# Seven-product down chunks in x's dead buffers, rotary angles on GpSimd, and one more Strassen pair in a two-layer trunk kernel

## The chip, the cores and the metric

The kernel runs on one core of one Trainium2 chip. The metric is device time in microseconds (us) of one execution, lower is better; several executions give a median. Engines are called by the profile's names: PE (TensorE, matrix multiply), PEld (its weight load), DVE (VectorE), ACT (ScalarE), POOL (GpSimd) and SP (the queue from which all DMAs of this kernel are issued).

## The reference, cut to what matters

Two layers, 256 positions, width 1024, fp32. The change touches the feed-forward halves (`ffn`, four in all) and the rotary tables of layer 1.

```python
def swiglu(h, w_gate, w_up, w_down):            # w_gate, w_up: 1024 x 2816; w_down: 2816 x 1024
    return (jax.nn.silu(h @ w_gate) * (h @ w_up)) @ w_down

def rope_tables(positions):
    ang = positions.astype(jnp.float32)[..., None] * inv_freq
    return jnp.cos(ang), jnp.sin(ang)

for i in range(2):
    x = x + 0.5 * swiglu(rmsnorm(x, ffn1_norm[i]), ffn1_w_gate[i], ffn1_w_up[i], ffn1_w_down[i])
    ...   # one input projection, self attention (relative bias in layer 0, differential with rotary in layer 1),
    ...   # cross attention into mem (256 x 1024), one output projection, added to x
    x = x + 0.5 * swiglu(rmsnorm(x, ffn2_norm[i]), ffn2_w_gate[i], ffn2_w_up[i], ffn2_w_down[i])
```

## The kernel before, in words

**Three passes per product.** Every dense product in fp32 is made of three PE matmuls of 128x512 in a reduced type: the high part of x by the high part of the weight, high by low, low by high (`dense`, lines 496, 499, 502). The weights arrive by DMA in fp32 as chunks of 128 x 2048 values (1 MB) in tile `raw` (three buffers). ACT casts a chunk to its high part `hi` (`split_hi`, line 326), DVE subtracts to get the low part `lo` (`split_lo`, line 344). `hi` and `lo` have four buffers each (pool `whl`), taken in turn, so a chunk can be split as soon as the buffer four takes back is free.

**Stages.** Each of the four `ffn` calls, (layer, which) = (0,1), (0,2), (1,1), (1,2), has a gate/up stage of 11 groups of 256 columns, two chunks a group, 24 matmuls a chunk, and then a down stage of 11 chunks, 24 matmuls a chunk. After a group, `evac` makes silu(gate)*up, transposes it in blocks (DVE), sends it through DRAM to turn it (`hd` out, `hr` back, lines 627 and 632) and splits it for the down stage (`ht`). The last three down chunks are done output quarter by output quarter, so that each quarter of x is finished, normalised and turned (`finish`, `prep_half`) while PE works on the next.

**Products by Strassen's scheme.** Where `PAIR[l, nm]` names a group, that group and the next are computed with seven products of four 12-matmul blocks instead of eight (Winograd's form): `pair_forms` makes four sums of x on DVE and splits them, `split_lo` makes sums of weight blocks (`wsum`, line 338), `pair_sums` adds the products up. Before, three of the four gate/up stages do it (from group 3) and the first, (0,1), does not. Where `SEVEN[l, nm]` names down chunks, each takes seven products instead of eight (`seven_item`, `seven_forms`, `seven`); such a chunk needs seven `hi`/`lo` quarters and so two of the four buffers; after the last one `seven_sums` adds the products into x (nine DVE operations, lines 690 and 695). The chunks are 1, 4, 6 in (0,2) and (1,1), and 1, 4, 7 in (1,2).

**Who sets the order.** All instructions are issued in an order that a planner at build time (class `Flow`) works out: it keeps a clock from fixed costs (a 128x512 matmul 0.216 us, a hop between engines 0.22 us), and threads yield the time or condition at which they go on. Each engine then runs its own instructions in that order and waits on semaphores. Ordinary threads go ahead of the idle ones (`loader`, `split_hi`, `split_lo`, `rope_setup`); many wait until DVE or ACT is free within `SLACK` = 0.4 us by the planner's clock. A split of the chunk that PE is working on does not wait for that.

**Rotary angles.** `rope_setup` computes the angles by a chain of 95 small dependent DVE operations on 128x64 or smaller (argument reduction in five pieces), then two `Sin` on ACT and 16 small DVE products. It is an idle thread and each operation goes only when DVE has nothing to do, so that the chain spreads from 125 us to 640 us of the profile; the tables are first used at 688 us. `memory_turn` and `memory_prep` bring `mem` in and turn it during (0,1).

Of the kernel before, what the change touches and what calls it, by code (L numbers as in the profile page):

```python
# [12 lines left out]
F32 = mybir.dt.float32  # L13
F32R = mybir.dt.float32r
# [6 lines left out]
P = 128  # L21
# [121 lines left out]
def kernel(  # L143
# [101 lines left out]
    class Item:  # L245
# [3 lines left out]
        def __init__(self, raws, uses=8, w=1):  # L249
# [3 lines left out]
            self.n, self.frees, self.takes, self.gives = 1, 1, 0, 0  # L253
# [15 lines left out]
    hl_left = [NHL]  # L269
    dma_free = [2.3]  # L270
# [94 lines left out]
    SEVEN = {(0, 1): (), (0, 2): (1, 4, 6), (1, 1): (1, 4, 6), (1, 2): (1, 4, 7)}  # L365
    PAIR = {(0, 1): None, (0, 2): 3, (1, 1): 3, (1, 2): 3}
# [10 lines left out]
    def seven_item(it):  # L377
# [3 lines left out]
        it.n, it.uses, it.takes, it.gives = 2, 7, 4, 4  # L381
# [48 lines left out]
    def plan_ffn(l, nm, wg, wu, wd):  # L430
# [58 lines left out]
    def dense(ps, xh, xl, ready, c, need, start, stop):  # L489
# [14 lines left out]
        if c.uses == 0:  # L504
            hl_left[0] += c.n
        return flow.pe(T_MM)
# [88 lines left out]
    def ffn(l, nm, xt, gc_next):  # L595
# [5 lines left out]
        def evac(g, ps, end, gives=None):  # L601
# [27 lines left out]
            g2.give()  # L629
            yield g2.has()  # L630
# [206 lines left out]
        nxt = None if gc_next is None else Xt(nm == 2 and PAIR[l + 1, 1] is not None)  # L837
# [27 lines left out]
        if nm == 1:  # L865
            table_hint(AF.Exp)
        for tb in range(2):
# [55 lines left out]
    def memory_turn():  # L923
        yield lambda: at[0] >= 8
        ss = const.tile([P, 2, 4], F32, name="mss")
        for q in range(4):
# [22 lines left out]
    def memory_prep():  # L949
        yield g2.has(8)  # L950
# [102 lines left out]
    def calm(n, extra=0.0):  # L1053
        t = flow.dve(n, extra) + 0.3
        return lambda: flow.now >= t and flow.free["V"] <= flow.now

    def rope_setup():
# [13 lines left out]
        nc.vector.tensor_copy(pf, pi)  # L1071
        yield calm(2)
        for tb in range(2):
            nc.vector.tensor_scalar(out=ang[:, tb * 32:(tb + 1) * 32], in0=invf, scalar1=pf[:, tb:tb + 1],
                                    scalar2=None, op0=ALU.mult)
            yield calm(n)
# [3 lines left out]
        nc.vector.tensor_copy(hi, hr.bitcast(F32))  # L1080
        yield calm(n)
        nc.vector.tensor_sub(lo, ang, hi)
        yield calm(n)
# [595 lines left out]
```

## Time and profile before

| | |
|---|---|
| median of 3 runs | 961.64 us (959.97 to 965.21) |
| profiled execution, its own time | 962.03 us |
| its span in the trace | 960.3 us |
| mean granted TensorE clock | 0.998 of 2.4 GHz |
| PE, DVE, ACT, POOL busy | 99%, 84%, 60%, 7% of the span |

The span runs from the first to the last instruction; 1.7 us of the profiled execution's time lie around it. A busy PE is not a PE at its peak, since matmuls overlap and their ends are modelled; the starts of successive matmuls tell how fast PE takes them.

### The profile page before, as it was taken

What the parts mean: (1) busy time and instruction counts of PE and PEld (TensorE: products, weight loads), DVE (VectorE), ACT (ScalarE), POOL (GpSimd) and SP (SyncE); (2) the same over time, 40 slices, a digit from 0 to 9 for tenths busy, and PEclk for the clock granted to TensorE, in tenths of its full rate; (3) what the DMA queues carried; (4) which work ended last, traced back from release to release, by engine and by line L of the source; (5) the groups of instructions that cost most, each with busy time, mean ns of one, the idle gap of its engine ahead of it and who ended that gap; (6) DMA issues with size and microseconds to landing.
All of it is one profiled execution on the core that took longest, in us unless ns stands there. A gap on an engine that the chain in (4) does not pass through costs nothing.

```text
span 960.3 us, 13252 instructions
## 1 busy us (share of the span) xinstructions
PE 948.0 (99%) x4489; PEld 776.9 (81%) x4489; DVE 806.0 (84%) x1532; ACT 577.8 (60%) x1100; POOL 63.1 (7%) x65
## 2 busy tenths in 40 slices
PE   8999999999999999999999999999999999999998
PEld 6888888888877888888888888887787788888886
DVE  6867777788877889979989988798989888997885
ACT  6655555566676656556646655554676866665651
POOL 1000000022110100000000000000334100000000
PEclk9999999999999999999999999999999999999999
DMA  8988868486435387786756678666541375688761
GB/s 275 332 256 273 278 229 274 154 272 210 158 107 174 92 262 226 233 289 221 234 184 201 219 231 263 221 234 224 187 165 45 126 223 183 211 258 261 240 230 44
DMA packets 169294, 204.02 MB, mean 212 GB/s; under 512 B 9674, under 2 KB 144395, under 8 KB 169227
## 3 DMA queue, kind: packets, MB, share of 16 engines
q1 hardware_dynamic: 169226, 203.18, 65.7%
q8 instruction: 35, 0.57, 0.2%
q14 instruction: 33, 0.26, 0.1%
HBM read 188.99 MB, written 14.16 MB: 212 GB/s over the span
## 4 chain that ended last, share of the span: by engine, by line
PE 87%; DVE 8%; DMA 2%; ACT 1%; SPq 1%; issue 1%; DVEq 0%; ACTq 0%
PE gu L502 14%; PE gu L499 14%; PE gu L496 14%; PE acc L496 8%; PE acc L502 8%; PE acc L499 8%; DVE lo L344 3%; PE pj L502 3%; PE pj L499 3%; PE pj L496 3%; PE pair_m L502 2%; PE pair_m L499 2%; PE pair_m L496 2%; PE xtp L509 1%; PE S L1320 1%; PE AV L1401 1%
## 5 line engine op out<-in xcount | busy, mean ns | idle before, releaser
L326 ACT CAST hi<-raw 128x512 fp32r<-128x512 f32 (+1 forms) x469 | 338.2, 771 | 160.9 <-DMA raw<-in_ffn_w_up_dram 43.4
L344 DVE TENSOR_TENSOR lo<-raw,hi 128x512 fp32r<-128x512 f32 (+1 forms) x469 | 393.0, 873 | 45.4 <-ACT hi L326 44.6
L502 PE MATMUL gu<-hi,xl 128*128 128x512 f32 x608 | 236.9, 390 | 0.0
L496 PE MATMUL gu<-hi,xh 128*128 128x512 f32 x608 | 236.8, 389 | 0.0
L499 PE MATMUL gu<-lo,xh 128*128 128x512 f32 x608 | 236.7, 389 | 0.0
L502 PEld LDWEIGHTS gu<-hi,xl 128*128 128x128 f32 x608 | 114.1, 188 | 23.7
L499 PEld LDWEIGHTS gu<-lo,xh 128*128 128x128 f32 x608 | 114.1, 188 | 23.6
L496 PEld LDWEIGHTS gu<-hi,xh 128*128 128x128 f32 x608 | 114.2, 188 | 23.5
L499 PE MATMUL acc<-lo,ht 128*128 128x512 f32 x280 | 110.1, 393 | 2.0 <-DVE lo L344 2.0
L496 PE MATMUL acc<-hi,ht 128*128 128x512 f32 x280 | 110.0, 393 | 0.0
L502 PE MATMUL acc<-hi,ht 128*128 128x512 f32 x280 | 109.9, 393 | 0.0
L502 PE MATMUL pj<-hi,xl 128*128 128x512 f32 x160 | 64.5, 403 | 0.0
L499 PEld LDWEIGHTS acc<-lo,ht 128*128 128x128 f32 x280 | 52.9, 189 | 13.7 <-DVE lo L344 2.9
L499 PE MATMUL pj<-lo,xh 128*128 128x512 f32 x160 | 63.6, 397 | 0.0
L496 PE MATMUL pj<-hi,xh 128*128 128x512 f32 x160 | 63.5, 397 | 0.0
L502 PEld LDWEIGHTS acc<-hi,ht 128*128 128x128 f32 x280 | 53.0, 189 | 11.0
L496 PEld LDWEIGHTS acc<-hi,ht 128*128 128x128 f32 x280 | 53.0, 189 | 10.9
L641 ACT CAST ht<-hr 128x512 fp32r<-128x512 f32 x35 | 21.7, 619 | 65.2 <-DMA hr<-hd 65.1
L326 ACT CAST hi<-wsum 128x512 fp32r<-128x512 f32 x84 | 49.2, 621 | 15.7 <-DVE wsum L338 12.3
L344 DVE TENSOR_TENSOR lo<-wsum,hi 128x512 fp32r<-128x512 f32 x84 | 53.0, 682 | 0.0
L610 ACT ACTIVATE sil<-gu,xr 128x256 f32<-128x256 f32 x76 | 35.7, 469 | 24.6 <-PE gu L502 24.1
L643 DVE TENSOR_TENSOR ht<-hr,ht 128x512 fp32r<-128x512 f32 x35 | 24.0, 687 | 26.1 <-ACT ht L641 26.0
(215 smaller groups left out, 1297.6 us busy)
## 6 DMA issues: line engine op xcount, KB each, us to landing
raw<-in_ffn_w_down_dram SPq DMA_DIRECT2D x176, 256.0 KB, 4.3
raw<-in_ffn_w_gate_dram SPq DMA_DIRECT2D x86, 512.0 KB, 4.6
raw<-in_ffn_w_up_dram SPq DMA_DIRECT2D x86, 512.0 KB, 5.7
raw<-in_w_in_dram SPq DMA_DIRECT2D x32, 512.0 KB, 5.9
hd<-hb SPq DMA_DIRECT2D x44, 256.0 KB, 4.9
hr<-hd SPq DMA_DIRECT2D x44, 256.0 KB, 3.7
raw<-in_w_out_dram SPq DMA_DIRECT2D x8, 1024.0 KB, 4.9
raw<-in_w_mem_kv_dram SPq DMA_DIRECT2D x4, 1024.0 KB, 5.6
```

Of the source, the lines that this page charges most:

```text
L326: nc.scalar.copy(out=it.part(0, q, w), in_=src())
L344: nc.vector.tensor_sub(it.part(1, q, w), src(), it.part(0, q, w).bitcast(F32))
L496: nc.tensor.matmul(out=ps, lhsT=xh, rhs=wh, start=start, stop=False)
L499: nc.tensor.matmul(out=ps, lhsT=xh, rhs=wl, start=False, stop=False)
L502: nc.tensor.matmul(out=ps, lhsT=xl, rhs=wh, start=False, stop=stop)
L509: nc.tensor.transpose(out=dst, in_=src, identity=flip if flipped else ident)
L610: nc.scalar.activation(sil, ps[tb][:, 0:256], AF.Silu, scale=xt.r[tb])
L641: nc.scalar.copy(out=hi, in_=src)
L643: nc.vector.tensor_sub(lo, src, hi.bitcast(F32))
L1320: nc.tensor.matmul(out=ss[e][:, pr, :nk], lhsT=q[rows, pr, :], rhs=k[rows, pr, :], start=i == 0, stop=i == len(passes) - 1)
L1401: nc.tensor.matmul(out=av[64 * e:64 * e + 64, pr, :], lhsT=vsrc(kb, pr, e), rhs=pts[e][:, pr, kb, :], start=(kb == 0), stop=(kb == nb - 1))
```

## The change

Five things are changed. (1) `PAIR[0, 1]` becomes 5: the first gate/up stage computes groups 5 and 6 by seven products. (2) `SEVEN` becomes 1, 4, 7 in (0,2) and (1,1). (3) Of the chunks in `SEVEN`, all but the first are guests: they take one `hi`/`lo` buffer instead of two, and their four summed quarters go to the buffers of the normalised x (`xh`, `xl`), which nobody reads in the down stage; a flag `xt_room` keeps one guest there at a time, and the next stage's x (`Xt`) is made after the eighth chunk instead of before the first. In the last three down chunks the second and third quarters are split in the other order. (4) The 95 operations on the angles go to POOL, where each is planned at 0.25 us and the next follows without waiting for an idle DVE. (5) The read-back of a turned group (`hr`) is planned 2 us later, and three conditions of waiting are changed.

```diff
-            t = (self.lo if lo else self.hi)[q // 4]
-            return t[:, q % 4 * 512:(q % 4 + w) * 512]
+            ts = self.lo if lo else self.hi
+            if self.guest and q >= 4:
+                return ts[q // 2 - 1].rearrange("p k t -> p (k t)")[:, q % 2 * 512:(q % 2 + w) * 512]
+            return ts[q // 4][:, q % 4 * 512:(q % 4 + w) * 512]
...
-            yield lambda: hl_left[0] >= it.n and all(r.raw is not None for r in it.raws)
+            yield lambda: (hl_left[0] >= it.n and all(r.raw is not None for r in it.raws)
+                           and (xt_room[0] or not it.guest))
             hl_left[0] -= it.n
+            if it.guest:
+                xt_room[0] = False
...
+            if it.guest:
+                for x, ts in (("xh", it.hi), ("xl", it.lo)):
+                    ts += [xtp.tile([P, KT, P], F32R, tag=f"{x}{j}", name=f"g{x}{j}") for j in range(2)]
...
-    SEVEN = {(0, 1): (), (0, 2): (1, 4, 6), (1, 1): (1, 4, 6), (1, 2): (1, 4, 7)}
-    PAIR = {(0, 1): None, (0, 2): 3, (1, 1): 3, (1, 2): 3}
+    SEVEN = {(0, 1): (), (0, 2): (1, 4, 7), (1, 1): (1, 4, 7), (1, 2): (1, 4, 7)}
+    PAIR = {(0, 1): 5, (0, 2): 3, (1, 1): 3, (1, 2): 3}
...
-        it.n, it.uses, it.takes, it.gives = 2, 7, 4, 4
+        it.n, it.uses, it.takes, it.gives, it.guest = 1 if guest else 2, 7, 4, 4, guest
...
-                seven_item(dn[-1])
+                seven_item(dn[-1], c != SEVEN[l, nm][0])
+            elif c >= NG - 3:
+                u = dn[-1].units
+                u[1], u[2] = u[2], u[1]
...
             hl_left[0] += c.n
+            xt_room[0] |= c.guest
...
             yield flow.now + 3.0
             g2.give()
+            yield flow.now + 2.0
             yield g2.has()
             hr = g2.take([P, 4, P], F32, "hr")
...
-        nxt = None if gc_next is None else Xt(nm == 2 and PAIR[l + 1, 1] is not None)
+        xt_room[0] = True
...
+        assert xt_room[0]
+        xt_room[0] = False
+        nxt = None if gc_next is None else Xt(nm == 2 and PAIR[l + 1, 1] is not None)
         for tb in range(2):
             flow.spawn(finish(acc, tb, nxt, gc_next, True))
...
-                yield lambda: flow.free["V"] <= flow.now
+                yield lambda: flow.free["V"] <= flow.now + SLACK
                 t = turn_blocks(xb[:, :, tb], m[:, tb])
...
     def memory_prep():
-        yield g2.has(8)
+        yield lambda: len(memd) == 4 and g2.left >= 8
...
             for part in (hi, lo):
-                nc.vector.tensor_scalar(out=a, in0=part, scalar1=float(cval), scalar2=None, op0=ALU.mult)
-                yield calm(n)
...
+                nc.gpsimd.tensor_scalar(out=a, in0=part, scalar1=float(cval), scalar2=None, op0=ALU.mult)
+                yield flow.pool(0.25)
...
-                    yield calm(n)
+                    flow.dve(n, 0.06)
+                    t = flow.dve(n, 0.06) + 0.3
+                    yield lambda: flow.now >= t and flow.free["V"] <= flow.now + SLACK
```

The other 91 operations of `rope_setup` are moved in the same way, from `nc.vector` with `calm` to `nc.gpsimd` with `flow.pool(0.25)`; the two `Sin` stay on ACT and the 16 products on DVE.

## Rows read from the trace of the kernel before

**Rows 1.** Page, part 1: busy time, share of the span, instructions.
```profile
PE 948.0 (99%) x4489; PEld 776.9 (81%) x4489; DVE 806.0 (84%) x1532; ACT 577.8 (60%) x1100; POOL 63.1 (7%) x65
```

**Rows 2.** Page, part 4: shares of the chain that ended last, by engine.
```profile
PE 87%; DVE 8%; DMA 2%; ACT 1%; SPq 1%; issue 1%; DVEq 0%; ACTq 0%
```

**Rows 3.** Stretches: length, busy us of PE, PEld, DVE, ACT, POOL; clock; DMA.
```profile
131.00:181.00 50.00, 50.00 (x222) 41.37 (x221) 36.48 (x95) 29.33 (x57) 0.00 (x0) 1.00 0.73 240
323.00:436.00 113.00, 113.00 (x502) 93.63 (x501) 103.05 (x169) 66.82 (x104) 0.93 (x1) 1.00 0.75 240
351.00:408.00 57.00, 57.00 (x253) 47.23 (x252) 53.06 (x86) 33.59 (x49) 0.00 (x0) 1.00 0.74 235
612.00:655.00 43.00, 43.00 (x192) 35.60 (x191) 40.53 (x79) 28.25 (x55) 0.00 (x0) 1.00 0.62 202
655.00:660.00 5.00, 2.99 (x13) 1.85 (x11) 4.96 (x9) 4.88 (x9) 0.00 (x0) 1.00 0.92 293
660.00:663.50 3.50, 3.50 (x9) 2.73 (x10) 3.49 (x6) 0.75 (x2) 0.00 (x0) 0.51 0.73 217
940.00:956.00 16.00, 16.00 (x72) 13.24 (x71) 8.55 (x14) 0.74 (x2) 0.00 (x0) 1.00 0.13 49
```

**Rows 4.** Timeline of PE, first gate/up stage: start, length, line, tiles.
```profile
39.84 0.39 PE L496 MATMUL gu<-hi,xh 128*128 128x512 f32 x1
...
42.56 0.39 PE L496 MATMUL gu<-hi,xh 128*128 128x512 f32 x1
```

**Rows 5.** Timeline of PE, end of the third down stage; bracketed: idle before, releaser.
```profile
656.58 0.39 PE L496 MATMUL acc<-hi,ht 128*128 128x512 f32 x1
...
658.13 0.50 PE L499 MATMUL acc<-lo,ht 128*128 128x512 f32 x1 [1.17 <-DVE lo L344]
...
659.94 0.69 PE L499 MATMUL acc<-lo,ht 128*128 128x512 f32 x1 [0.85 <-DVE lo L344]
...
663.42 0.43 PE L496 MATMUL acc<-hi,ht 128*128 128x512 f32 x1
```

**Rows 6.** Timeline of DVE, the same stretch.
```profile
656.79 0.69 DVE L695 TENSOR_TENSOR msum<-msum,m 128x512 f32<-128x512 f32 x1
657.39 0.69 DVE L344 TENSOR_TENSOR lo<-raw,hi 128x512 fp32r<-128x512 f32 x1
657.99 0.69 DVE L690 SCALAR_TENSOR_TENSOR x<-msum,x 128x512 f32<-128x512 f32 x1
```

**Rows 7.** Timeline of ACT, the same stretch.
```profile
654.77 2.19 ACT L326 CAST hi<-raw 128x512 fp32r<-128x512 f32 x4 [2.77 <-DMA raw<-in_ffn_w_down_dram]
```

**Rows 8.** Waits of the SP queue: us in total, times, longest.
```profile
SPq L632 <- DMA hd<-hb: 109.9, 35, 6.0
```

**Rows 9.** Groups by form: busy us, mean ns; then the idle time before.
```profile
L344 DVE TENSOR_TENSOR lo<-raw,hi 128x1024 fp32r<-128x1024 f32 x166 | 198.5, 1216 | 21.6 <-ACT hi L326 21.0 <-DMA raw<-in_ffn_w_gate_dram 0.3
...
L344 DVE TENSOR_TENSOR lo<-wsum,hi 128x512 fp32r<-128x512 f32 x84 | 53.0, 682 | 0.0
```

**Rows 10.** Timeline of DVE, start of the program.
```profile
16.72 1.29 DVE L344 TENSOR_TENSOR lo<-raw,hi 128x512 fp32r<-128x512 f32 x2
```

**Rows 11.** Timeline of PE, start of the program.
```profile
18.30 0.39 PE L499 MATMUL gu<-lo,xh 128*128 128x512 f32 x1
```

**Rows 12.** Groups by form of POOL.
```profile
L200 POOL TENSOR_SCALAR_AFFINE_SELECT flip<-flip 128x128 f32<-128x128 f32 x1 | 0.3, 292 | 0.1
```

**Rows 13.** Line 516 on POOL: duration min/median/max in ns, first and last start.
```profile
L516 POOL TENSOR_TENSOR xr<-v,nhalf x12: 548/796/1637, 20.1 to 792.3; 128x1 f32<-128x1 f32 x12
```

**Rows 14.** Timeline of POOL, second mixer.
```profile
688.04 2.12 POOL L1219 TENSOR_TENSOR m<-qkn,ropeS 128x256 f32<-128x256 f32 x2 [1.68 <-ACT hi L326]
```

**Rows 15.** Timeline of DVE, second mixer.
```profile
686.48 0.68 DVE L344 TENSOR_TENSOR lo<-raw,hi 128x512 fp32r<-128x512 f32 x1
...
689.49 1.22 DVE L344 TENSOR_TENSOR lo<-raw,hi 128x512 fp32r<-128x512 f32 x1
```

**Rows 16.** Tile ropew (rotary angles), first down stage: DVE and ACT busy.
```profile
131.00:181.00 50.00, 5.20 (x26) 0.00 (x0) 1.00 0.73 240
```

More of the change, by code (lines that the diff above doesn't have):

```diff
@@ L252, in __init__ @@
             self.hit, self.lot, self.st = [None] * 7, [None] * 7, [None] * 4
-            self.n, self.frees, self.takes, self.gives = 1, 1, 0, 0
+            self.n, self.frees, self.takes, self.gives, self.guest = 1, 1, 0, 0, False
             self.sums, self.t = [], []
@@ L269 @@
     hl_left = [NHL]
+    xt_room = [False]
     dma_free = [2.3]
@@ L375, with seven_item @@
     WO = (0, 1, 2, 3)
-    def seven_item(it):
+    def seven_item(it, guest):
         r = [it.own(q) for q in range(4)]
         t = lambda j: lambda: it.t[j]
-        it.n, it.uses, it.takes, it.gives = 2, 7, 4, 4
+        it.n, it.uses, it.takes, it.gives, it.guest = 1 if guest else 2, 7, 4, 4, guest
         it.sums = [(r[1], r[0]), (r[3], t(0)), (r[3], r[1]), (r[2], t(1))]
@@ L1051 @@
     nlam = const.tile([P, 1], F32, name="nlam")
-    def calm(n, extra=0.0):
-        t = flow.dve(n, extra) + 0.3
-        return lambda: flow.now >= t and flow.free["V"] <= flow.now
     def rope_setup():
@@ L1070, in rope_setup @@
         pf = const.tile([P, 2], F32, name="pos_f")
-        nc.vector.tensor_copy(pf, pi)
-        yield calm(2)
+        nc.gpsimd.tensor_copy(pf, pi)
+        yield flow.pool(0.25)
         for tb in range(2):
-            nc.vector.tensor_scalar(out=ang[:, tb * 32:(tb + 1) * 32], in0=invf, scalar1=pf[:, tb:tb + 1],
+            nc.gpsimd.tensor_scalar(out=ang[:, tb * 32:(tb + 1) * 32], in0=invf, scalar1=pf[:, tb:tb + 1],
                                     scalar2=None, op0=ALU.mult)
-            yield calm(n)
+            yield flow.pool(0.25)
         hr = const.tile([P, n], F32R, name="ropehr")
@@ L1079, in rope_setup @@
         yield flow.act(n)
-        nc.vector.tensor_copy(hi, hr.bitcast(F32))
-        yield calm(n)
-        nc.vector.tensor_sub(lo, ang, hi)
-        yield calm(n)
+        nc.gpsimd.tensor_copy(hi, hr.bitcast(F32))
+        yield flow.pool(0.25)
+        nc.gpsimd.tensor_sub(lo, ang, hi)
+        yield flow.pool(0.25)
         def frac(dst, src):
-            nc.vector.tensor_scalar(out=b, in0=src, scalar1=MAGIC, scalar2=MAGIC, op0=ALU.add, op1=ALU.subtract)
-            yield calm(n)
-            nc.vector.tensor_sub(dst, src, b)
-            yield calm(n)
+            nc.gpsimd.tensor_scalar(out=b, in0=src, scalar1=MAGIC, scalar2=MAGIC, op0=ALU.add, op1=ALU.subtract)
+            yield flow.pool(0.25)
+            nc.gpsimd.tensor_sub(dst, src, b)
+            yield flow.pool(0.25)
         left = Fraction(TWO_PI_INV_NUM, TWO_PI_INV_DEN)
@@ L1097, in rope_setup @@
             for part in (hi, lo):
[L1098 to L1105 removed]
+                nc.gpsimd.tensor_scalar(out=a, in0=part, scalar1=float(cval), scalar2=None, op0=ALU.mult)
+                yield flow.pool(0.25)
+                nc.gpsimd.tensor_scalar(out=fa, in0=a, scalar1=2.0 ** -12, scalar2=MAGIC, op0=ALU.mult, op1=ALU.add)
+                yield flow.pool(0.25)
+                nc.gpsimd.tensor_scalar(out=fa, in0=fa, scalar1=MAGIC, scalar2=4096.0, op0=ALU.subtract, op1=ALU.mult)
+                yield flow.pool(0.25)
+                nc.gpsimd.tensor_sub(a, a, fa)
+                yield flow.pool(0.25)
                 if first:
@@ L1110, in rope_setup @@
                     yield from frac(fa, a)
-                    nc.vector.tensor_add(acc, acc, fa)
-                    yield calm(n)
+                    nc.gpsimd.tensor_add(acc, acc, fa)
+                    yield flow.pool(0.25)
                     yield from frac(acc, acc)
         S2PI = 6.283185
-        nc.vector.tensor_scalar(out=a, in0=acc, scalar1=0.25, scalar2=None, op0=ALU.add)
-        yield calm(n)
+        nc.gpsimd.tensor_scalar(out=a, in0=acc, scalar1=0.25, scalar2=None, op0=ALU.add)
+        yield flow.pool(0.25)
         yield from frac(a, a)
```

8 lines of the change are left out of this document (removed).

## The prediction

> **What bounds the kernel now.** I read the page's busy shares and its chain first: PE is busy 99% of the span [rows 1] and holds 87% of the chain [rows 2]. So only two things move the time: how many matmuls PE issues, and where it stands still. The timeline gives the price of a matmul: twelve are issued in 42.56 - 39.84 = 2.72 us [rows 4], 0.227 us each. Then the stretches: in the first down stage, in the gate/up stage of (0,2), which already has a Strassen pair, and in the last quarter of the kernel, PE is busy for the whole stretch [rows 3], so nothing the other engines do there reaches the end. One stretch differs, the end of the down stage of (1,1): from 655 to 660 us PE is busy 2.99 of 5 us, and in the 3.5 us behind it at a granted clock of 0.51, that is 1.2 instead of 2.4 GHz [rows 3]. The timeline says why: PE waits 1.17 and 0.85 us for `lo` on DVE [rows 5]. Twelve matmuls lie between the starts at 656.58 and 663.42, 6.84 us where the pitch gives 2.72: 4.12 us are lost, more in waiting, the rest at the lower clock.
>
> What was late there is read on two engines. DVE alternates splits of the last weight chunk with additions of `seven_sums` [rows 6], 0.60 us from one to the next, so every second operation is not for the waiting PE. ACT had sat 2.77 us until that chunk landed [rows 7], and its load could only go when chunk 7's `raw` buffer came free behind DVE. DVE is busy 40.53 of 43 us in this stage [rows 3].
>
> **The change, part by part.**
>
> *Strassen in (0,1).* Four 24-matmul chunks become seven products of 12: 96 - 84 = 12 matmuls fewer, 2.72 us [rows 4], direct on the path. It costs DVE four sums and four splits of x, sixteen weight sums, sixteen plus six splits for eight, and seven sums of products. With 0.63 us for a 512-wide and 1.20 us for a 1024-wide operation (53.0/84 and 198.5/166 [rows 9]) that is 47 x 0.63 - 2 x 1.20 = 27 us of DVE. What hides it is the same load in (0,2): with such a pair DVE is busy 103.05 of 113 us and PE 113.00 of 113, and 53.06 of 57 us while the pair runs [rows 3]. In (0,1) the eight block transposes of `mem` come on top. The cover is thin in one place, the start. There the low parts of the second chunk's third and fourth quarters are written from 16.72 in 1.29 us [rows 10], the third in half of that, by 17.4, and the matmul that reads it begins at 18.30 [rows 11]: 0.9 us of lead. `pair_forms` becomes ready just then with four sums in a row. By the planner's rule PE's own chunk goes first; then the sums delay only the third chunk. If they come first, four times 0.60 us [rows 6] less 0.9 is 1.5 us of stall. I take 0.3 and keep 0 to 1.5.
>
> *Chunks 1, 4, 7 with guests.* No matmul is added or removed. A guest takes one buffer of four instead of two, so the plain chunks behind it can be split one chunk, 24 x 0.227 = 5.4 us, earlier. The last chunk then waits for chunk 6's buffer and for its load, no longer for half of a seven-product chunk. `seven_sums` starts one chunk later and now falls right into the last three chunks; but the stage of (1,2) has these chunks already, and PE is busy 16.00 of its last 16 us with DVE at 8.55 [rows 3]. The new wait is the guest's own: chunk 7 cannot start its split before chunk 4 has been multiplied, and everything behind it in ACT's and DVE's order waits too. PE then has chunks 5 and 6, 48 x 0.227 = 10.9 us, against seven splits, 7 x 0.63 = 4.4 us behind sums that need no buffer. That holds. I take the whole 4.12 us as gained, bounds 0 and 4.12. The later `Xt` costs nothing: its first write follows the first finished quarter, after the last guest.
>
> *`hr` 2 us later.* SP waited 109.9 us, 35 times, 3.1 us each, for the way out before it could issue the way back [rows 8], with weight loads queued behind. Two us less of that lets loads pass; it is part of why I expect (1,1) to recover. The turned group arrives later but is used tens of us on. I count 0.
>
> *Angles on POOL.* DVE loses 95 short operations, 5.20 us of them in the first down stage [rows 16], where PE did not wait anyway. On POOL the trace has no 128x64 operation. From below, a one-input 128x128 takes 0.29 us [rows 12]; from above, a two-input 128x256 takes 2.12/2 = 1.06 us [rows 14], and a 128x1 power, whatever its own arithmetic, spreads from 0.55 to 1.64 [rows 13], so something beside the element count adds up to half a microsecond. It is DVE: a 512-wide split that takes 0.68 us takes 1.22 [rows 15] while POOL multiplies [rows 14]. I take 0.5 us, nearer the one-input row since over half of these operations have one input and all have at most 64 elements. The chain is then 95 x 0.5 = 48 us. The planner steps 0.25 + 0.22 = 0.47 us each, 45 us by its clock, 47 us on the chip since its matmul is 0.216 and the real one 0.227. Real and planned agree within a us. That matters because of a new wait: `Sin` stands in ACT's order where the plan ends the chain. If POOL is late, ACT stops there, and behind it the casts of the down weights, DVE's splits, and PE. The cover is the splits' lead. ACT may be three chunks ahead of PE, 16.3 us, less one cast and one split, so 15 us, and ACT and DVE with 29.33 and 36.48 of 50 us [rows 3] can be that far ahead. I count 0. Were the cover gone, each 0.1 us on the POOL operation would cost 9.5 us.
>
> The Trainium skill ("SBUF — State Buffer", section "SBUF: two separate sides") says that DVE operations with two SBUF inputs and GpSimd operations that read SBUF take one shared port pair by an exclusive lock for the whole instruction. The row at 1.22 us agrees; what it does to this chain is the third rival below.
>
> *Sum*, against the profiled execution's own 962.03 us: 962.03 - 2.72 - 4.12 + 0.3 = **955.5 us**. That execution lies 0.4 us above the median of the runs shown, 961.64, less than their scatter, so I leave the number.
>
> **The rivals.**
>
> 1. *The stall in (1,1) stays or only moves.* For it: DVE is busy 94% of that stage, the guest brings no DVE work away, and the sums now fall on the very last chunks. Against: (1,2) with the same sums has no stall, and DVE is rid of what was left of the rotary chain. Then 962.03 - 2.72 + 0.3 = 959.6, with half of it 957.5.
>
> 2. *The first stage pays back its gain.* For it: 0.9 us of lead at the start, 27 us more DVE work, transposes of `mem` squeezed in. A stall of 1.5 us at the start and as much again in the pair, or a dip of the clock like that of [rows 3], gives 955.2 + 3 = 958.2.
>
> 3. *The POOL chain runs late and ACT stops at `Sin`: slower.* If each POOL operation first waits out a DVE operation and then holds it up, 0.3 us become 0.3 + 0.63 = 0.93. The chain is then 95 x 0.93 = 88 us, 41 us behind the plan, and 41 - 15 = 26 us of stall: 981. It decides from (47 + 15)/95 = 0.65 us each, and outdoes the gains from (47 + 15 + 6.5)/95 = 0.72. Against it: DVE is busy 73% of that stage [rows 3], so a POOL operation often finds it idle or waits only a remainder, half of 0.63 on average; 0.3 + 0.73 x 0.32 = 0.53.
> By that lock rule of the Trainium skill the worst case would be the 0.93; the spread of the powers bears out some waiting, not a full one each time.
>
> 4. *More is gained than counted.* DVE is relieved a little in both mixers, where PE has short waits. I have no row that prices it; I allow 2 to 3 us, 953.
>
> **How the numbers follow.** Chances: forecast 0.54 (its own range 954 to 957), rival 1 0.18, rival 2 0.13, rival 3 0.08, rival 4 0.07. The range 952.5 to 960.5 takes in the forecast, rivals 1 and 2, and most of rival 4, and leaves out rival 3 and tails, under 2 in 10. About 0.5% (4.8 us) is what a measurement of this kernel tells from no change; from 962.03 that is 957.2. Faster: forecast, rival 4, and a few of rival 1 and 2, 0.60. Same: the rest of 1 and 2 and a mildly late POOL, 0.33. Slower: rival 3 well past its limit, 0.07.
>
> **What would show it.** The matmul count falls by 12 from the 4489 of PE [rows 1]. PE has no wait for `lo` in the last 15 us of the down stage of (1,1), and the granted clock no half-speed stretch there. The pair in (0,1) shows PE busy throughout. POOL has 95 more instructions, and their mean says whether 0.5 us held; ACT's idle time before `Sin` says whether rival 3 bit. The prediction is wrong if PE waits appear in the first 25 us, around the pair of (0,1), at chunk 7 of (0,2) or (1,1), or where memory's keys are projected behind the first down stage, should `mem` be turned too late.

## The result and the profile after

The changed kernel takes 962.99 us (960.49 to 968.99, 20 runs) against 960.00 us (958.24 to 965.21, 20 runs) for the kernel before: ratio 1.0028, 95% interval 1.0016 to 1.0040. I had forecast 955.5, with 952.5 to 960.5. It is 0.28% slower, where I had expected 0.7% faster.

Of all runs of the kernel before that accompany the experiments, the 91 with a mean granted clock of 0.999 or more have a median of 959.9 us and the 58 with less one of 962.8, and the profiled execution from which I worked (962.03 us, clock 0.998) is of the second kind: 3.4 us at half speed [rows 3] lower the mean by 0.002.

The page of the changed kernel's profiled execution (960.92 us, span 959.1), part 1:

```profile
PE 946.6 (99%) x4477; PEld 773.9 (81%) x4477; DVE 821.0 (86%) x1482; ACT 587.6 (61%) x1121; POOL 113.2 (12%) x160
```

PE has the twelve matmuls fewer, 4477 against 4489 [rows 1], POOL 95 instructions more. DVE has 50 instructions fewer and yet 15 us more work: short ones left, 512-wide ones came. The chain that ended last has moved in part from PE to what feeds it (87, 8 and 2% for PE, DVE and DMA before [rows 2]):

```profile
PE 78%; DVE 11%; DMA 6%; ACT 3%; issue 1%; SPq 1%; DVEq 0%; ACTq 0%
```

Stretches of the changed kernel (length, busy us of PE, PEld, DVE, ACT, POOL; clock; DMA):

```profile
13.00:131.00 118.00, 117.04 (x512) 95.05 (x511) 103.67 (x162) 71.87 (x119) 5.87 (x7) 1.00 0.80 253
131.00:181.00 50.00, 48.78 (x216) 40.06 (x215) 41.14 (x78) 33.93 (x68) 34.06 (x67) 1.00 0.87 292
612.00:655.00 43.00, 43.00 (x192) 35.59 (x191) 38.88 (x69) 29.70 (x56) 0.00 (x0) 1.00 0.75 236
655.00:670.00 15.00, 15.00 (x72) 12.43 (x71) 10.57 (x17) 4.30 (x10) 0.00 (x0) 1.00 0.31 88
```

The kernel before in the first of these:

```profile
13.00:131.00 118.00, 118.00 (x523) 97.47 (x523) 88.24 (x138) 67.79 (x110) 4.94 (x4) 1.00 0.90 282
```

The end of the down stage of (1,1) is what I hoped for: PE is busy 15.00 of 15 us at full clock, where it had stood at 655 to 660 us [rows 3, 5]. The new loss is at the front, where PE had no wait before: 117.04 of 118 us in the gate/up stage of (0,1), 48.78 of 50 in its down stage [rows 3]. PE's waits in the changed kernel (us in total, times, longest):

```profile
...
PE acc L511 <- DVE lo L353: 1.2, 1, 1.2
PE pair_m L511 <- DVE v L527: 0.8, 1, 0.8
...
PE gu L511 <- DVE lo L353: 0.2, 1, 0.2
```

Their places, from PE's timeline (the pair's last product; the second down chunk):

```profile
120.74 0.39 PE L508 MATMUL pair_m<-hi,xh 128*128 128x512 f32 x1
121.89 0.50 PE L511 MATMUL pair_m<-lo,xh 128*128 128x512 f32 x1 [0.76 <-DVE v L527]
...
136.75 0.39 PE L508 MATMUL acc<-hi,ht 128*128 128x512 f32 x1
138.36 0.50 PE L511 MATMUL acc<-lo,ht 128*128 128x512 f32 x1 [1.22 <-DVE lo L353]
```

DVE before the first of them:

```profile
115.36 1.10 DVE L936 STREAM_TRANSPOSE mb<-mem 128x256 f32<-128x256 f32 x2
116.38 0.45 DVE L626 SCALAR_TENSOR_TENSOR h<-gu,xr,sil 128x256 f32<-128x256 f32 x1
116.74 1.29 DVE L347 TENSOR_TENSOR wsum<-raw,wsum 128x512 f32<-128x512 f32 x2
117.94 0.45 DVE L634 STREAM_TRANSPOSE hb<-h 128x256 f32<-128x256 f32 x1
118.30 0.66 DVE L784 TENSOR_TENSOR gu_u<-gu_u,pair_m 128x512 f32<-128x512 f32 x1
118.88 1.29 DVE L347 TENSOR_TENSOR wsum<-raw,wsum 128x512 f32<-128x512 f32 x2
120.07 0.69 DVE L657 TENSOR_TENSOR ht<-hr,ht 128x512 fp32r<-128x512 f32 x1
...
121.14 0.69 DVE L353 TENSOR_TENSOR lo<-wsum,hi 128x512 fp32r<-128x512 f32 x1
```

There is no idle time in this list: transposes of `mem`, sums of weights, sums of products and the turned group stand ahead of the `lo` for which PE waits. (The releaser is given as `v`, a short instruction right behind that `lo`.) And ACT, which casts ahead of DVE, had itself stood still for weights:

```profile
97.17 1.05 ACT L335 CAST hi<-raw 128x1024 fp32r<-128x1024 f32 x1 [4.17 <-DMA raw<-in_ffn_w_up_dram]
...
130.27 1.14 ACT L335 CAST hi<-raw 128x512 fp32r<-128x512 f32 x2 [4.17 <-DMA raw<-in_ffn_w_down_dram]
```

The reason is on the SP queue: the loads go out late. The first two chunks of down weights, in the changed kernel and then in the kernel before:

```profile
115.14 2.67 SPq L291 DMA_DIRECT2D raw<-in_ffn_w_down_dram  x4
...
123.53 2.56 SPq L291 DMA_DIRECT2D raw<-in_ffn_w_down_dram  x4
```

```profile
102.80 2.67 SPq L288 DMA_DIRECT2D raw<-in_ffn_w_down_dram  x4
...
108.58 2.56 SPq L288 DMA_DIRECT2D raw<-in_ffn_w_down_dram  x4
```

They go 12 and 15 us later, and ACT's waits for up weights between 13 and 131 us grow from 5.1 to 18.1 us. The waits of SP in that time, changed kernel and kernel before:

```profile
SPq L291 <- DVE lo L353: 34.4, 14, 5.3
SPq L646 <- DMA hd<-hb: 18.6, 5, 4.8
```

```profile
SPq L288 <- DVE hb L621: 19.9, 8, 3.4
SPq L288 <- DVE h L613: 19.1, 7, 4.0
SPq L288 <- DVE lo L344: 11.2, 5, 3.6
SPq L632 <- DMA hd<-hb: 8.0, 6, 2.5
```

The line with `lo` alone seems to triple, but taken over all operations of DVE the loads waited 40.6 us against 52.8 before. So it is not the sum of the waits that tells of a late DVE, it is the starts of the loads: a late split frees its `raw` buffer late. What did grow in sum is the read-backs that hold the queue in front of loads (8.0 to 18.6 us).

For the experiments I use stage lengths, each from the first matmul of a stage in the trace to the first of the next (us):

| kernel | gate/up (0,1) | down (0,1) | mixer 0 | down (0,2) | down (1,1) | mixer 1 |
|---|---|---|---|---|---|---|
| before | 121.39 | 61.27 | 103.37 | 59.25 | 63.41 | 104.94 |
| changed | 120.84 | 63.11 | 104.78 | 59.25 | 59.25 | 104.70 |

The other stages agree within 0.4 us in these two. Twelve matmuls fewer should have made the first 118.67; it is 2.2 above that, the second is 1.8 and the mixer 1.4 above before.

### The profile page after: what moved, and what is told of

It reads as the page before. It is cut to its first block, busy times and chain, and to the rows that moved or that the text cites. A ratio compares the mean times of both kernels' runs of the same rounds, so it can differ in the third digit from the quotient of the medians.

```text
span 959.1 us, 13289 instructions
## 1 busy us (share of the span) xinstructions
PE 946.6 (99%) x4477; PEld 773.9 (81%) x4477; DVE 821.0 (86%) x1482; ACT 587.6 (61%) x1121; POOL 113.2 (12%) x160
## 4 chain that ended last, share of the span: by engine, by line
PE 78%; DVE 11%; DMA 6%; ACT 3%; issue 1%; SPq 1%; DVEq 0%; ACTq 0%
PE gu L514 12%; PE gu L511 11%; PE gu L508 11%; PE acc L508 7%; PE acc L514 7%; PE acc L511 7%; DVE lo L353 5%; PE pj L514 2%; PE pj L511 2%; PE pj L508 2%; PE pair_m L514 2%; PE pair_m L511 2%; PE pair_m L508 2%; DMA raw<-in_ffn_w_up_dram 2%; DMA raw<-in_ffn_w_down_dram 2%
## 5 line engine op out<-in xcount | busy, mean ns | idle before, releaser
L514 PE MATMUL gu<-hi,xl 128*128 128x512 f32 x576 | 224.5, 390 | 0.4 <-DVE xl L559 0.4
L511 PE MATMUL gu<-lo,xh 128*128 128x512 f32 x576 | 224.6, 390 | 0.2 <-DVE lo L353 0.2
L508 PE MATMUL gu<-hi,xh 128*128 128x512 f32 x576 | 224.4, 390 | 0.0
L511 PEld LDWEIGHTS gu<-lo,xh 128*128 128x128 f32 x576 | 108.1, 188 | 23.8 <-DVE lo L353 1.2
L514 PEld LDWEIGHTS gu<-hi,xl 128*128 128x128 f32 x576 | 108.1, 188 | 22.8 <-DVE xl L559 0.8
L508 PEld LDWEIGHTS gu<-hi,xh 128*128 128x128 f32 x576 | 108.1, 188 | 22.3
L529 POOL TENSOR_TENSOR xr<-v,nhalf 128x1 f32<-128x1 f32 x12 | 10.4, 870 | 428.2 <-DVE v L527 428.2
L623 ACT ACTIVATE sil<-gu,xr 128x256 f32<-128x256 f32 x72 | 33.7, 468 | 25.9 <-PE gu L514 23.4
L529 POOL TENSOR_TENSOR hf<-v,nhalf 128x8 f32<-128x8 f32 (+1 forms) x20 | 31.5, 1576 | 91.5 <-DVE v L527 80.1
```

The lines of the kernel that those rows point to most:

```text
L508: nc.tensor.matmul(out=ps, lhsT=xh, rhs=wh, start=start, stop=False)
L511: nc.tensor.matmul(out=ps, lhsT=xh, rhs=wl, start=False, stop=False)
L514: nc.tensor.matmul(out=ps, lhsT=xl, rhs=wh, start=False, stop=stop)
L529: nc.gpsimd.tensor_tensor(out=dst, in0=v[:, :n], in1=nhalf[:, :n], op=ALU.pow)
L623: nc.scalar.activation(sil, ps[tb][:, 0:256], AF.Silu, scale=xt.r[tb])
```

## The experiments

**First, undo one part, or do one alone.** Theory A of the expectations is that the pair leaves DVE short of time in its stage; the rivals stand beside it there.

`no_pair01`, the changed kernel with

```diff
-    PAIR = {(0, 1): 5, (0, 2): 3, (1, 1): 3, (1, 2): 3}
+    PAIR = {(0, 1): None, (0, 2): 3, (1, 1): 3, (1, 2): 3}
```

> The changed kernel without the Strassen pair in the first gate/up stage; all else stays, and the 12 matmuls (2.72 us) come back. Theory A, the pair costs more in that stage than it saves, because DVE is short there (its splits fall from 14 us ahead of PE to 0.1): this kernel is 2 to 5 us faster than the changed one, 958 to 961 us, at or below the kernel before. Theory B, the loss comes from the angles on POOL, the later read-back or the other order of the down chunks: this kernel is 2.7 us slower than the changed one, 965.7 us. In the trace A expects splits 13 to 14 us ahead through the first gate/up stage and no PE gap over 0.5 us between 15 and 140 us.

Measured 956.98 us (956.60 to 958.37), ratio 0.9964 [0.9952, 0.9975]. The first two stages are 121.30 and 61.27, mixer 0 is 103.32. So the pair costs 6.0 us. That is theory A, and 1 us more than its range. The traces show 3.4 of them (960.92 against 957.51 in the profiled executions): (120.84 - 121.30) + (63.11 - 61.27) + (104.78 - 103.32) = 2.84 us in three stages, 0.2 in mixer 1 and the start, the rest behind the last matmul. The other 2.6 lie between medians and profiled executions (the changed kernel's was 2.1 us under its median, this one's 0.5 above); in which stage, no trace shows.

`pair_alone`, the kernel before with the pair alone (and memory's preparation waiting for all four quarters of `mem`):

```diff
-    PAIR = {(0, 1): None, (0, 2): 3, (1, 1): 3, (1, 2): 3}
+    PAIR = {(0, 1): 5, (0, 2): 3, (1, 1): 3, (1, 2): 3}
...
-        yield g2.has(8)
+        yield lambda: len(memd) == 4 and g2.left >= 8
```

> The kernel before with the pair in the first gate/up stage alone (and the guard that memory_prep waits for all four quarters of mem). Theory A: slower than before by 1 to 4 us, 961 to 964 us, with PE gaps near 23 us and near 120 us. Theory B: faster than before by the 12 matmuls, 2.7 us, 957.3 us.

Measured 964.16 us (962.44 to 969.42), ratio 1.0046 [1.0027, 1.0066]. First stage 119.27, but the first down stage 64.62 and the stage of memory's keys 29.18 instead of 22.25: `mem` was turned from idle moments of DVE that no longer came, the last transpose at 175 us (before: 118).

`old_sevens`, the changed kernel without guests (`SEVEN` 1, 4, 6 and the order of quarters as before):

```diff
-    SEVEN = {(0, 1): (), (0, 2): (1, 4, 7), (1, 1): (1, 4, 7), (1, 2): (1, 4, 7)}
+    SEVEN = {(0, 1): (), (0, 2): (1, 4, 6), (1, 1): (1, 4, 6), (1, 2): (1, 4, 7)}
...
-                seven_item(dn[-1], c != SEVEN[l, nm][0])
-            elif c >= NG - 3:
-                u = dn[-1].units
-                u[1], u[2] = u[2], u[1]
+                seven_item(dn[-1], False)
```

> The changed kernel with the seven-product chunks 1, 4, 6 again in (0,2) and (1,1), two buffers each and the old order of quarters. If the guests removed the stall at the end of the down stage of (1,1), it comes back here: 1 to 4 us slower than the changed kernel, 964 to 967 us, and PE waits for lo there. If that stall was only one of the ways in which runs of the kernel before differ, the two are within 0.5 us, 963 us.

Measured 961.95 us (959.62 to 965.22), ratio 1.0013 [1.0001, 1.0026], no worse than the changed kernel. The down stage of (1,1) is 59.25 here too: its waits go without the guests. (The first down stage is 65.12 in this trace, with a wait for `lo` of 1.93 us.)

`hr_at_once`, the changed kernel without the later read-back:

```diff
             g2.give()
-            yield flow.now + 2.0
             yield g2.has()
```

> The changed kernel with the read-back of a turned group planned 2 us earlier, as before. If the later read-back keeps SP free for weight loads, this is slower by 0.5 to 3 us, 963.5 to 966 us, with more waiting of SP for the way out. If the delay starves the first stage, it is 0.5 to 2 us faster, 961 to 962.5 us. If it does neither, 963 us.

Measured 966.38 us (964.75 to 967.42), ratio 1.0060 [1.0042, 1.0079]. SP waits 135.1 us in 40 read-backs, against 64.1 us in 23 in the changed kernel; first two stages 122.47 and 65.03. So the later read-back helps the changed kernel, a little more than the first of the three expectations has it.

**Second, what is short in the first stage.** `before_again` is the kernel before once more, for its trace; `no_pair_old_sevens` leaves only the angles on POOL and the later read-back.

> The kernel before, once more, with a profile. If the stall at the end of the down stage of (1,1) belongs to this kernel's order, the stage is again about 63.4 us long with PE waits for lo over 1 us, and the time is near 962 us. If it belongs to that one execution, the stage is 59.3 us as in the other kernels with the old chunks, and the time is 957 to 960 us.

963.06 us, (1,1) 63.23 us: the waits at its end come again, with the half-speed stretch behind them.

> The changed kernel with neither the pair in the first stage nor the guests: chunks 1, 4, 6 with two buffers, old order of quarters; what is left of the change is the angles on POOL and the later read-back. If the guests are what took the stall out of (1,1), this is 1 to 3 us slower than the kernel without the pair (956.98), 958 to 960 us. If the later read-back and the relieved DVE did it, it is within 0.5 us of 957 us.

957.67 us (957.06 to 960.75), ratio 0.9971 [0.9958, 0.9984]: most of the gain of `no_pair01` is there without the guests; the time lies between the two that were expected.

`mem_turn_off_dve`, the changed kernel with the eight transposes of `mem` left out (POOL writes a constant instead; memory's keys are then not the reference's):

```diff
-                yield lambda: flow.free["V"] <= flow.now + SLACK
-                t = turn_blocks(xb[:, :, tb], m[:, tb])
+                nc.gpsimd.memset(xb[:, :, tb], 0.5)
+                t = flow.pool(0.5)
```

> The changed kernel with the eight block transposes of mem in the first stage left out (a POOL memset writes their tile instead), about 5 us of DVE less in and around the pair; attention to mem reads constants. Theory A, DVE is short there: the splits stay ahead at the end of the pair, the PE gaps near 121 and 137 us (2.3 us in the profile) go, 1.5 to 4 us faster than the changed kernel, 959 to 961.5 us. Rival: what is short is the three raw buffers, two of which the pair holds, and the way round them (5 us of load, cast, split): no change beyond 0.7 us, 963 us.

956.83 us (954.95 to 958.74), ratio 0.9961 [0.9945, 0.9977]: 6.2 us less than the changed kernel, for eight operations of about 0.6 us. In the trace the first two stages and mixer 0 are 119.23, 61.26 and 103.60. The stretch from 13 to 131 us:

```profile
13.00:131.00 118.00, 117.87 (x519) 96.71 (x518) 105.19 (x166) 77.16 (x129) 10.68 (x19) 1.00 0.86 275
```

DVE is busy for longer than in the changed kernel, 105.19 against 103.67 us, and PE almost throughout. I read this so: it was not DVE's total that was short but its time ahead of certain splits, and when these are late DVE stands too. The edit also shifts the planned order, so how much of the 6.2 us is the transposes' own work isn't shown; moving half of them behind the pair, below, gave less.

`late_forms`, the changed kernel with the four sums of x held back until chunk 6:

```diff
-            yield lambda: len(xt.y) == 4 and g4.left >= 4
+            yield lambda: len(xt.y) == 4 and g4.left >= 4 and ((l, nm) != (0, 1) or at[0] >= 6)
```

> The changed kernel with the sums of x for the pair made only when PE has reached the seventh chunk, not in the first 25 us. If the start pays (my 0 to 1.5 us), the gap near 23 us goes and it is 0.3 to 1 us faster than the changed kernel, 962 to 962.7 us, and 2 us faster if the lost lead at the start is what is missing at the end of the pair. If the lead is won back before the pair anyway, no more than 0.5 us.

960.45 us (958.04 to 961.42), ratio 1.0000 [0.9990, 1.0011]: 2.5 us less than the changed kernel. The waits at 23 us go, those at 120 and 125 us stay (first stage 120.87); the first down stage is back at 61.27.

**Third, each remaining part alone, and the pair placed better.** `hr_alone` is the kernel before with `yield flow.now + 2.0` ahead of the read-back; `rope_alone` the kernel before with the angles on POOL; in `mem_after_pair` memory is turned from chunk 14 on, and `mem_after_pair_late_forms` has the delay of `late_forms` too:

```diff
     def memory_turn():
-        yield lambda: at[0] >= 8
+        yield lambda: at[0] >= 14
```

> The kernel before with one change: the read-back of a turned group is planned 2.0 us later. Theory B (the later read-back lets weight loads pass and so takes the waits for lo at the end of the down stage of (1,1) away): that stage falls from 63.4 to about 59.3 us, and the median is 1.5 to 3 us below the kernel before, as with both this and the angles on POOL (2.2 us below). Rival C (the angles on POOL do it, since DVE gets rid of the last of the chain there): the stage stays at 61 to 63.4 us and the median within 1 us of the kernel before. Rival D (any shift of the planned order does it): the stage also falls here, and in the next run, which has only the angles moved, too.

957.54 us (957.08 to 961.44), ratio 0.9966 [0.9954, 0.9978]; (1,1) 59.25.

> The kernel before with one change: the 95 operations on the angles go to POOL. Theory B: the end of the down stage of (1,1) still has PE waiting for lo, stage 61 to 63.4 us, median within 1 us of the kernel before. Rival C: the stage falls to about 59.3 us and the median is 1.5 to 3 us lower. Rival D: as C, but with the run before showing the same. On either view the first mixer may lose up to 1.4 us, if it is the angles' tables that are made on DVE there.

957.65 us (957.25 to 958.42), ratio 0.9970 [0.9958, 0.9982]; (1,1) 59.25. So rival D: either does it.

> The changed kernel with one condition moved: mem is brought in and turned from chunk 14 of the first gate/up stage on, behind the pair, and no longer from chunk 8. Nothing is left out. Theory A (DVE is short while pair and transposes of mem fall together): PE's waits at 120 to 125 and at 137 us go, the first gate/up stage falls from 120.8 to about 119 us, the first down stage from 63.1 to 61.3, and the median lies 3 to 5 us below the changed kernel, 958 to 960. Against it: the transposes now meet the split of the last chunks and the angles, and memory's keys may come late (a kv stage above 22.3 us); then it is at 962 or more.

960.60 us (957.68 to 964.43), ratio 0.9993 [0.9980, 1.0006]. The first stage is 119.25 as theory A has it, but the down stage 63.79, with a wait for `lo` of 2.23 us, and mixer 0 106.94; the median falls by 2.4 us, not 3 to 5. The name says more than the edit does: the products of the pair run from 65.4 to 122.7 us, and four of the eight transposes (at 92.79 and 110.74 us) still fall among them.

> The run before this one with the second delay too: the sums of x for the pair wait until chunk 6. Theory A: the two delays take away different shortages (the start, and the pair with mem), so their gains add: 2.5 us from the sums, 3 to 5 from mem, median 955 to 957.5, level with or below the version without the pair (956.98). If the first 25 us did not matter, it equals the run before. If DVE is simply too full for the pair wherever the work is put, both stay at 960 or above.

958.68 us (956.79 to 963.73), ratio 0.9983 [0.9970, 0.9997]. First two stages 118.66 and 61.29: the full price of twelve matmuls, 2.7 us. Mixers of 105.86 and 106.01 took it back, and the median is above the 955 to 957.5 that were expected.

**Fourth, where the rest goes.** `guests_alone` is the kernel before with the guests and the changed conditions of memory's threads. In the other two `rope_setup` waits until `ffn(0, 2)` is called; `pair_tables_later` is otherwise `mem_after_pair_late_forms`, `no_pair_tables_later` is `no_pair01`.

```diff
         yield from loaded()
+        yield lambda: second[0]
         yield g2.has()
...
         xt = mixer(l, xt, GC_FFN2 + l * KT)
+        second[0] = True
```

> The kernel before with the guests alone: chunks 1, 4, 7 in (0,2) and (1,1) and x's buffers for them, two of the changed conditions of memory's threads with it, no pair in (0,1), the angles on DVE, the read-back as before. The later read-back alone and the angles on POOL alone each took the waits of (1,1) away and gave 3.3 us. If the guests do it by the buffer that they save, and likewise if any shift of the planned order does it, the down stage of (1,1) falls to 59.3 us and the median to about 957.5. If the guests do nothing for it (the sums fall on the last chunks instead), the stage stays above 61 us and the median within 1 us of the kernel before. They cannot be told apart from each other by this run, only from the last.

958.59 us (957.14 to 961.71), ratio 0.9969 [0.9949, 0.9988]; (1,1) 59.25, with 1.2 us lost at the end of the first down stage (62.46).

> The changed kernel with the two delays (sums of x from chunk 6, mem from chunk 14) and the chain of angles on POOL begun only when the second ffn of layer 0 begins. The pair then keeps 2.7 us in the first two stages, but gave 2.5 us back in the first mixer (105.9 against 103.3 us without the pair). Theory E (the angles' tables, finished late beside the first mixer, are what costs there): the mixer falls to about 103.4 us and the median to 955.5 to 957. Theory F (the mixer's length is set by how the planned order happens to fall there, not by the tables): the mixer stays anywhere between 103.3 and 106 us, and the median between 956 and 959.

957.62 us (955.93 to 961.41), ratio 0.9956 [0.9936, 0.9977]; mixer 0 103.33, as theory E has it, though the median is 0.6 us above E's range.

> The changed kernel without the pair of (0,1) and with the chain of angles on POOL begun only when the second ffn of layer 0 begins. Theory E: nothing to gain, since the mixer is at 103.3 us already; median 956.5 to 957.5. Theory F: the mixer may change by 0 to 2 us although no work in it was added, median 957 to 959. If the angles on POOL held up the first down stage, that would show as a gain below 956.5.

958.06 us (957.07 to 960.21), ratio 0.9970 [0.9949, 0.9989]; mixer 0 103.32; the median fits F better. Against E stand two kernels of above: `rope_alone` and `no_pair_old_sevens` both finish the tables at 219 us, and their mixers take 103.37 and 104.75.

In `pair_tables_later` one wait of PE is left in front, 1.37 us for `lo` at 130.16. Its cause is two engines away, on the SP queue, where the load of a chunk goes out right behind a read-back that had waited 3.1 us:

```profile
119.56 0.37 SPq L646 DMA_DIRECT2D hr<-hd  x1
119.99 2.55 SPq L291 DMA_DIRECT2D raw<-in_ffn_w_down_dram  x4
```

and ACT sits until that chunk lands (its timeline):

```profile
126.70 0.62 ACT L335 CAST hi<-raw 128x512 fp32r<-128x512 f32 x1 [6.94 <-DMA raw<-in_ffn_w_down_dram]
```

**Fifth, that queue.** `pair_tables_hr4` and `pair_tables_hr3` are `pair_tables_later` with 4.0 and 3.0 in place of 2.0 ahead of the read-back; `no_pair_tables_hr4` is `no_pair_tables_later` with 4.0.

> The run pair_tables_later with the read-back of a turned group planned 4.0 us later instead of 2.0. There PE waits 1.4 us at 130 us, behind ACT, which sat 6.9 us until a chunk of down weights landed; the load went out at 120.0, right behind a read-back that had held the queue for 3.1 us. Theory G (the held queue is what makes the chunk late): the first down stage falls from 62.9 to about 61.3 us and the median to 955.5 to 957. Theory H (the chunk's raw buffer comes free no earlier, since DVE is late with the last splits of the pair): the stage stays at 62.5 or more and the median at 957 to 958.5.

955.87 us (954.46 to 959.87), ratio 0.9955 [0.9938, 0.9973], first down stage 61.27: theory G. The load now goes ahead of the read-back (SP queue, then ACT), and ACT waits 1.74 us:

```profile
117.35 2.56 SPq L291 DMA_DIRECT2D raw<-in_ffn_w_down_dram  x4
...
120.64 0.38 SPq L646 DMA_DIRECT2D hr<-hd  x1
```

```profile
124.27 0.62 ACT L335 CAST hi<-raw 128x512 fp32r<-128x512 f32 x1 [1.74 <-DMA raw<-in_ffn_w_down_dram]
```

> As the run before this one with 3.0 us instead of 4.0. Theory G: most of the 1.6 us is recovered too, since the wait was 3.1 us and shrinks by 1; first down stage 61.3 to 62, median 956 to 957.5. Theory H: no change, 957 to 958.5. If the two delays give results that differ by more than a microsecond in stages that neither touches, the planned order alone is worth that much.

962.21 us (958.65 to 966.59), ratio 1.0009 [0.9985, 1.0032]: a miss for the number, 63.48 us in the first down stage, since here the order put the read-back ahead of the load again (it stood 3.7 us), and ACT waited 4.06 us for the load (SP queue):

```profile
121.73 0.37 SPq L646 DMA_DIRECT2D hr<-hd  x1
122.15 2.55 SPq L291 DMA_DIRECT2D raw<-in_ffn_w_down_dram  x4
```

And another stage, down (0,2), went from 59.25 to 63.17 us; the delay holds for the read-backs of all four halves, so the order is planned anew there too. There PE waits 2.06 us, at 485.63, for a quarter of x that stands on DVE behind splits of the next stage, and the first of these had waited for its weights (timeline of DVE):

```profile
481.13 1.22 DVE L353 TENSOR_TENSOR lo<-raw,hi 128x1024 fp32r<-128x1024 f32 x1 [2.81 <-ACT hi L335]
...
483.67 1.22 DVE L353 TENSOR_TENSOR lo<-raw,hi 128x1024 fp32r<-128x1024 f32 x1
484.81 0.68 DVE L596 SCALAR_TENSOR_TENSOR x<-acc,x 128x512 f32<-128x512 f32 x1
```

Behind that wait eight matmuls start 0.43 us apart instead of 0.227 (granted clock 0.58 from 485.60 to 489.50 us).

The traces of all eleven kernels with the pair agree that the late chunk is what PE waits for, when sorted by how far ahead of the first down matmul the load of the second chunk of down weights goes out. In the five with 8.9 us or more (`mem_after_pair_late_forms` 8.9, `pair_alone` 9.6, `late_forms` 10.4, `pair_tables_hr4` 10.5, `mem_turn_off_dve` 15.2) PE never waits for `lo` in the first down stage; in the six with 7.7 or less (`pair_tables_later` 7.7, `old_sevens` 7.4, the changed kernel and `pair_tables_hr3` 7.1, `mem_after_pair` 6.1, `hr_at_once` 5.0) it waits 1.2 to 2.2 us.

> The best version (955.87 us, read-back 4.0 us later, angles from the second ffn on) without the pair of (0,1); mem is turned from chunk 8 again. If the pair is worth its twelve matmuls once nothing waits, this one is 2 to 2.7 us above, 957.9 to 958.6, with a first gate/up stage of 121.1 to 121.4 us against 118.8. If the later read-back alone made the best version, this one is level with it or below, 954 to 956.

958.24 us (957.15 to 960.03), ratio 0.9966 [0.9949, 0.9982]; first stage 121.95 against 118.81 with the pair. In the medians the pair is now worth 2.4 us, by the two ratios 1.1 us, and their intervals overlap: its gain is clear in the first stage and not shown in the whole. `pair_tables_hr4` has the lowest median of all.

## Why the prediction was wrong, by its own steps

**The base.** I summed from 962.03 us and left it. The median is 960.0: the profiled execution held a half-speed stretch [rows 3], and the mean clocks say that most executions have none. This error flattered the forecast. I forecast a change of -6.5 us and measured +3.0, a miss of 9.5; the high base, by luck, makes it 7.5 in the time itself.

**Strassen in (0,1): the step that failed.** The 2.72 us are real: 121.30 against 118.66 us once nothing waits. What failed is the cover, "the same load in (0,2)", with 0.3 us and a bound of 1.5 for the start. The pair cost 6.0 us where I had it at -2.42, so with its saving taken back it brought 8.7 us of loss. Three differences to (0,2) are in the traces. The lead is only 0.9 us at the start of this stage, as I had read; holding back the four sums there gave 2.5 us (`late_forms`), where I had priced them at 0.3, and the stage that became shorter is the down stage behind. The transposes of `mem` fall into the pair: I named them and gave them no price, and without them 6.2 us come back (2.4 where half of them were moved behind it). And a late split makes loads late: the first down weights go out 12 us later than before, and that I did not have at all. Rival 2 named this stage, but allowed a stall of 3 us. As a list of places the last sentence of the prediction was right: waits came in the first 25 us and around the pair; the down stage behind it I had not named.

**Guests.** The waits of (1,1) went, as forecast, and with them the half-speed stretch; but not by the guests' buffer. The read-back alone, the angles alone and the guests alone each end them, for 3.4, 3.3 and 2.3 us by their medians, about 3 us by each ratio; together without the pair they give 3.8. So the 4.12 us was over by about a quarter against the median; some 1.7 of it lies in eight matmuls at half speed (0.43 us apart instead of 0.227), which by their mean clocks most executions do not have. The cause that I gave, one buffer less, is not shown, but the late load that I read in [rows 7] is: in the kernel before the last chunk's load goes out at 648.04, 35.7 us into the stage, and in `hr_alone`, `rope_alone` and `guests_alone` 30.9, 30.5 and 28.5 us into theirs. ACT's cast of that chunk then no longer waits for a DMA. Between its splits DVE still works on the sums in `hr_alone` and `rope_alone`, in the same row as before, only some 3 us earlier in the stage. Why three different shifts of the order each free that buffer earlier stays open.

**`hr`, counted at 0.** In the changed kernel it is worth 3.4 us (966.38 against 962.99), as I read it because the queue is in front of the loads that the pair made urgent (135.1 against 64.1 us of waiting for the way out).

**Angles on POOL.** In the first down stage my 0.5 us held: 94 operations from 126.5 to 200.6 us of 0.51 us on average, 0.47 without the pair. The chain was not 48 us long but 74, since it first waited 13.9 us for ACT's cast of the angles and its operations follow each other with gaps. ACT did not wait for POOL at `Sin` (202.14 us, the last of the chain begins at 200.6): rival 3 did not bite. Something of its mechanism shows all the same: begun in (0,2), where DVE is busy 104.99 of 113 us, the same operations take 0.67 us and ACT waits 0.5 and 2.0 us at the two `Sin` (that stretch and ACT's timeline, `pair_tables_later`):

```profile
323.00:436.00 113.00, 113.00 (x500) 93.50 (x500) 104.99 (x169) 64.78 (x101) 59.40 (x88) 1.00 0.75 236
```

```profile
387.28 0.26 ACT L1133 ACTIVATE ropew<-ropew 128x64 f32<-128x64 f32 x1 [0.51 <-POOL ropew L1102]
389.51 0.26 ACT L1134 ACTIVATE ropew<-ropew 128x64 f32<-128x64 f32 x1 [1.98 <-POOL ropew L1102]
```

PE loses nothing there, 113.00 of 113, as the lead of the splits covers it. What I had not looked at lies behind `Sin`: the products on DVE that make the tables run into mixer 0, to 226 us in the changed kernel. Mixers with tables in them took 103.3 to 106.9 us, those without 103.3 to 104.1 (`no_pair_tables_hr4`). So tables may cost there, but the order alone moves this stage by 0.8 us or more, and their share stays open.

**The account.** From 960.0: everything but the pair, mostly the waits of (1,1), -3.0 (`no_pair01`), the pair +6.0; 963.0 was measured. Of the miss of 9.5 us the pair holds 8.4 and the waits of (1,1) 1.1. Where in the kernel 2.6 of the pair's 6.0 us fall isn't shown, nor what lengthens mixer 0.

## What to carry to other kernels

A scheme that takes work from the bound engine must be priced in the stage where it is put: count the lead that the feeding engines have when it starts, and whatever else they do there, not the same load in a later stage. Three unrelated edits each moved the time by 2 to 4 us in the same place, and a planned delay of 2, 3 or 4 us by up to 6, so where an order is fixed at build time an edit must be tried beside neighbours that only shift it. Ask of a queue what stands behind each instruction that waits: here a read-back held 1 MB of weights, and the price appeared three engines later.

## What the hardware showed that I had not expected

In these traces a POOL operation takes longer beside a busier DVE. The same 128x64 operations took 0.47 us on average in a first down stage with DVE busy 35.36 of 50 us (`no_pair01`), 0.51 with 41.14 (changed kernel) and 0.67 in (0,2) with 104.99 of 113; long ones there run beside a split on DVE (POOL, then DVE, `pair_tables_later`):

```profile
338.88 1.28 POOL L1100 TENSOR_SCALAR ropew<-ropew 128x64 f32<-128x64 f32 x1
340.25 1.27 POOL L1102 TENSOR_TENSOR ropew<-ropew 128x64 f32<-128x64 f32 x1
341.50 0.37 POOL L1112 TENSOR_SCALAR ropew<-ropew 128x64 f32<-128x64 f32 x1
```

```profile
340.16 1.18 DVE L353 TENSOR_TENSOR lo<-raw,hi 128x1024 fp32r<-128x1024 f32 x1
341.27 0.47 DVE L626 SCALAR_TENSOR_TENSOR h<-gu,xr,sil 128x256 f32<-128x256 f32 x1
341.66 1.21 DVE L353 TENSOR_TENSOR lo<-raw,hi 128x1024 fp32r<-128x1024 f32 x1
```

The operation at 340.25 runs beside the split of 340.16 to 341.34 and ends at 341.52; the same line (L1102) takes 0.32 us at least and 0.45 in the median in this trace. The one at 338.88 stands likewise beside a split, of 338.54 to 339.88. The Trainium skill ("SBUF — State Buffer", section "SBUF: two separate sides") has an exclusive lock between GpSimd operations that read SBUF and DVE operations with two SBUF inputs; this trace agrees, with 1.27 us against 0.32 to 0.45.

In this kernel a wait for a DMA costs the loads behind it, not only its own reader: a read-back that stood 3.1 us at 119.56 us sent 1 MB of weights out at 119.99, and ACT sat 6.94 us for it. The Trainium skill ("DMA: Bandwidth & Descriptors", section "Anatomy of one DMA — SWDGE (gpsimd) path") notes that a DMA's wait for a semaphore happens on the sequencer that issues it, before dispatch; its account is of DMAs issued from GpSimd, and the order of the two starts on the SP queue agrees.

A wait of PE of about 2 us was followed by a half-speed stretch in some places and not in others. Behind 2.06 us in `pair_tables_hr3` and 1.93 us in `old_sevens` eight matmuls start 0.43 us apart; behind 2.23 us in `mem_after_pair` (clock 1.00 from 131.70 to 136.00 us) and behind another 1.90 us in `pair_tables_hr3` none do. What decides it, these traces don't show.
